# Sums of squares from GpSimd to VectorE, and half of the attention's probability scaling from VectorE to ScalarE

## The chip, the core and the metric

The kernel is one launch on one core of a Trainium2 chip. The metric is device microseconds of that launch, the median of several runs. A second source is one profiled execution, whose trace says when each instruction ran, what it waited for and which TensorE clock was granted. Engines are called as the profile calls them: PE is TensorE's matrix multiply and PEld its weight load, DVE is VectorE, ACT is ScalarE, POOL is GpSimd, SP is SyncE, which issues the DMAs. Columns of 128 partitions by W elements are written 128xW; everything here is float32.

## The reference, cut to what matters

A two-layer streaming encoder step on 1024 prompt frames and 32 sample frames (1056 columns), model width 1024. Layer 0 is a gated linear recurrence (HGRN2) and a SwiGLU feed-forward network; layer 1 is sliding-window attention with sinks and a second feed-forward network. Every sub-layer has a normalization before and after it. The change touches two computations:

```python
def rms_norm(x, w):
    xf = x.astype(F32)
    y = xf * lax.rsqrt(jnp.mean(xf * xf, axis=-1, keepdims=True) + NORM_EPS)
    return (y * w.astype(F32)).astype(x.dtype)
...
    p = jnp.exp(s - m)
    denom = jnp.sum(p, axis=-1, keepdims=True) + jnp.exp(sink - m)
    return jnp.einsum('bnkgqs,bnskd->bnqkgd', p / denom, v.astype(F32))
```

The first is a mean of squares over 1024 features, the second the division of the attention's exponentials by their sum.

## The kernel before, in words

Activations lie feature-major: eight tiles of 128 features, each with the columns of one of three blocks b of 384, 384 and 288 columns. Weights come by DMA as 128x1024 units; ACT rounds each to a high part `wh` (L102, or L98 with a scale per partition) and DVE takes the rest as a low part `wl` (L103, L99). Activations are split the same way into `xh` (ACT, L217 or L220) and `xl` (DVE, L218 or L221). A product then takes three passes on PE, high by high, high by low and low by high: L141 and L153 for projections, L416 and L141 in the first half of a feed-forward network, L507 in its second half. Products land in tiles tagged `mm`, of which there are four in PSUM.

**Sums of squares.** `sq_acc` (L176) is called once for each of the eight feature tiles of a block. The first call squares straight into an accumulator `acc` (ACT, L178). Each of the other seven squares into a scratch tile `q` (ACT, L181) and adds `q` to `acc` on POOL (L182). When all eight are in, `rnorm` (L184) sums over the 128 partitions with a matmul by ones (L188) and takes an inverse root with short ACT and DVE steps (L191, L192, L163 to L171). There are 24 such sums, so 168 adds: in `xload` (the input's pre-norm, three blocks), in `outproj` (six), in `postnorm` where a next norm follows (nine), and in the last loop of `ffn` (six, L593). In `postnorm`, each tile is scaled (L251), the residual is added (L252), the result split (L217, L218) and squared. In the last loop of `ffn`, a product tile is added into `mix` from PSUM (L592) and then squared.

**Attention.** `att_s` (L1249) handles one KV head g, its four query heads and one chunk of 128 (or 32) queries: 36 chunks. PE makes the scores (L1272, masks L1282), DVE takes row maxima (L1285, L1290, L1291), ACT exponentiates the four heads with row sums (L1294) and the sink (L1296), DVE adds the sink (L1297), takes the reciprocal (L1298) and multiplies all four heads at once by it, broadcast along the keys (L1299). `att_t` (L1303) then transposes the four heads on PE in the order 0 to 3 (L1312), ACT and DVE copy the transposes out (L1317, L1319), and `att_v` (L1322) multiplies by the values (L1330) and splits the result (L1332, L1333). The loop at L1392 calls `att_s` for chunk u, some projection work from the plan, and only then `att_t` and `att_v` for chunk u-1.

**Order.** The program writes tile operations; the order of each engine's queue is planned when it is built, from the dependencies, the order written and the builder's own estimates of durations, and then stays fixed. Each engine works through its queue in order. `rnorm`'s matmul is tied into PE's queue behind the last dense matmul written before it (`after_dense`, L156), so that PE waits there if the sum is not ready.

```python
        with after_dense():
            nc.tensor.matmul(ps[:, :W], ones, acc[:, :W], start=True, stop=True)
```

Of the kernel before, what the change touches and what calls it, by code (L numbers as in the profile page):

```python
# [13 lines left out]
AF = mybir.ActivationFunctionType  # L14
# [45 lines left out]
def build(nc, tc, I, O):  # L60
    ctx = ExitStack()
    mult, add, sub, mn = ALU.mult, ALU.add, ALU.subtract, ALU.min
# [20 lines left out]
    def tmp(bufs=4):  # L83
        return tp.tile([128, 384], F32, tag="tmp", name="tmp", bufs=bufs)
# [91 lines left out]
    def sq_acc(acc, W, src, first):  # L176
        if first:
            nc.scalar.activation(acc[:, :W], src, AF.Square)  # L178
        else:
            q = tmp()  # L180
            nc.scalar.activation(q[:, :W], src, AF.Square)  # L181
            nc.gpsimd.tensor_tensor(acc[:, :W], acc[:, :W], q[:, :W], add)  # L182

    def rnorm(acc, dst, W, ps=None):  # L184

# [37 lines left out]
    def postnorm(b, mix, acc, w2, xold, wnext, spill, yout, done, more=None, full=None):  # L223
# [25 lines left out]
        for k in range(KT):  # L249
            m = mix[:, k, :]  # L250
            nc.vector.scalar_tensor_tensor(m, m, pcol(w2, k), rb2[:, :W], mult, mult)  # L251
            nc.vector.tensor_tensor(m, m, xos[k][:, :W], add)  # L252
            load()
            if yout is None:
                if full is None:
                    put_x(b, k, m, xs, wnext)
                sq_acc(nacc, W, m, k == 0)
            if k % 2:
                nc.sync.dma_start(dst[:, k - 1:k + 1, :], mix[:, k - 1:k + 1, :])
                if k < KT - 1:  # L260
                    yield
# [962 lines left out]
    with tc.tile_pool(name="aps", bufs=1, space=PSUM, reuse_waits="tile") as aps:  # L1224
# [24 lines left out]
        def att_s(b, g, jl):  # L1249
            j = 3 * b + jl  # L1250
            samp = j == 8
            rows = 32 if samp else 128
            qs = slice(jl * 128, jl * 128 + rows)
            kb = kbs[b]
            if samp:
                keys = [(kc, 0, 128), (kb, 384, 32)]
                vals = [(vc, 128), (vts[8], 32)]
                lo, kend = 0, 160
            elif j == 0:
                keys, vals, lo, kend = [(kb, 128, 128)], [(vts[0], 128)], 128, 256  # L1260
            else:
                keys, vals, lo, kend = [(kb, jl * 128, 256)], [(vts[j - 1], 128), (vts[j], 128)], 0, 256
# [25 lines left out]
            rs = ap2.tile([128, 4], F32, tag="rs", name="rs", bufs=2)  # L1288
# [3 lines left out]
            P = ap2.tile([128, 4, 256], F32, tag="P", name="P", bufs=2)  # L1292
            for hh in (0, 2, 1, 3):
# [2 lines left out]
            nc.scalar.activation(es[:rows], es[:rows], AF.Exp)  # L1296
            nc.vector.tensor_tensor(rs[:rows], rs[:rows], es[:rows], add)  # L1297
            nc.vector.reciprocal(rs[:rows], rs[:rows])  # L1298
            nc.vector.tensor_tensor(P[:rows, :, lo:kend], P[:rows, :, lo:kend],  # L1299
                                    rs[:rows].unsqueeze(2).broadcast_to([rows, 4, kend - lo]), mult)  # L1300
            return dict(b=b, g=g, rows=rows, qs=qs, vals=vals, lo=lo, P=P)

        def att_t(c):  # L1303
# [76 lines left out]
        for b in range(NB):  # L1380
            if b == 1:
                kload(2)
                close(rpc)
                mbc, mb = pool("mb1", "right")

                def mtag(b):
                    return f"mixb{b}"

                mbs[:] = [mb, mb, None]
            os[b] = newx(b)  # L1390
            prev = None
            for u in range(13):  # L1392
                c = att_s(b, u // 3, u % 3) if u < 12 else None
                if u % 3 == 0 and u > 0 and order:
                    qload()
                for f, n in plan[b].get(u, ()):
                    go(f, n)
                if prev is not None:
                    att_t(prev)
                    att_v(prev)  # L1400
                prev = c
# [112 lines left out]
```

## Time and profile before

| | |
|---|---|
| median of 3 runs (lowest, highest) | 2544.05 us (2542.91, 2549.28) |
| the profiled execution's own time | 2548.6 us |
| its span, first to last instruction | 2546.8 us |
| PE busy | 2469.6 us (97%) |
| DVE busy | 1722.0 us (68%) |
| ACT busy | 1101.2 us (43%) |
| POOL busy | 457.5 us (18%) |
| mean granted TensorE clock | 0.988 |

The chain of waits follows the work that ended last back to its releasers; a group is all instructions of one line, engine and shape; "idle before" is an engine's idle time just ahead of an instruction, with what ended it. A window row gives, for one stretch: its length, then the busy time and count of PE, PEld, DVE, ACT and POOL, the granted clock (1.00 is full speed), the DMA share and GB/s. A timeline row gives start, duration, engine, line, operation, tiles, shapes, count and the idle time before it; consecutive instructions of one kind are merged into one row.

### The profile page before, as it was taken

The page shows a single profiled execution, that of the slowest core. Times are in us where ns is not written, and L with a number is a line of the kernel's source. Part 1 is how long each engine was busy: PE and PEld are TensorE (multiplying, and loading weights), DVE is VectorE, ACT ScalarE, POOL GpSimd, SP SyncE. Part 2 cuts the span into 40 slices and gives each one's busy share as a digit, 9 for nine tenths or more (in the row PEclk, how much of TensorE's full clock was granted, in tenths as well). Part 3 has the DMA queues.
Part 4 walks back from the last instruction along what each step waited for, and adds up shares of the span by engine and source line. Part 5 has one row for each costly group of instructions (what it writes and reads, how often), then busy time and mean ns, then how long its engine had stood idle before and what let it go on. Part 6 is the DMA issues. An engine that isn't in the chain of part 4 may idle for free.

```text
span 2546.8 us, 44040 instructions
## 1 busy us (share of the span) xinstructions
PE 2469.6 (97%) x17124; PEld 2373.7 (93%) x17124; DVE 1722.0 (68%) x3510; ACT 1101.2 (43%) x2395; POOL 457.5 (18%) x644
## 2 busy tenths in 40 slices
PE   7999998999999999999998999999999999999997
PEld 7999998998899999999998997777999999999997
DVE  8788789888776666643467747787776666652456
ACT  6555565666533333341344424565533333342333
POOL 4443444332300000000033321121300000000012
PEclk9999999999999999999999999998999999999998
DMA  5233334343422222242445542332422222252455
GB/s 171 91 101 99 115 110 138 124 135 107 156 72 82 80 77 76 78 166 77 150 158 165 181 128 63 86 120 70 162 80 76 76 76 77 77 177 76 147 168 156
DMA packets 124153, 287.98 MB, mean 113 GB/s; under 512 B 13432, under 2 KB 68632, under 8 KB 123944
## 3 DMA queue, kind: packets, MB, share of 16 engines
q1 hardware_dynamic: 123944, 285.17, 34.9%
q8 instruction: 134, 2.20, 0.3%
q14 instruction: 75, 0.61, 0.1%
HBM read 237.25 MB, written 48.07 MB: 112 GB/s over the span
## 4 chain that ended last, share of the span: by engine, by line
PE 74%; DVE 12%; DMA 5%; ACT 4%; issue 3%; POOL 1%; SPq 0%; POOLq 0%; DVEq 0%; ACTq 0%
PE mm L141 23%; PE mm L507 18%; PE mm L416 14%; PE c L416 6%; PE mm L153 5%; DVE wl L103 2%; PE sc L1272 2%; PE pav L1330 1%; ACT wh L102 1%; PE ptp L1312 1%; DVE wl L99 1%; DMA wst<-in_wfq 1%; DMA xl<-g 1%; DVE mixb L252 1%; DMA xo<-in_x 1%
## 5 line engine op out<-in xcount | busy, mean ns | idle before, releaser
L141 PE MATMUL mm<-xh,wh 128*128 128x384 f32 (+1 forms) x1968 | 632.9, 322 | 11.1 <-ACT xh L220 7.5
L141 PE MATMUL mm<-xh,wl 128*128 128x384 f32 (+1 forms) x1968 | 624.3, 317 | 5.5 <-DVE wl L99 3.0
L141 PE MATMUL mm<-xl,wh 128*128 128x384 f32 (+1 forms) x1968 | 627.1, 319 | 2.0 <-DVE xl L221 1.3
L182 POOL TENSOR_TENSOR acc<-acc,tmp 128x384 f32<-128x384 f32 (+1 forms) x168 | 211.3, 1262 | 1693.7 <-ACT tmp L181 1669.4
L103 DVE TENSOR_TENSOR wl<-wst,wh 128x1024 fp32r<-128x1024 f32 (+1 forms) x301 | 379.3, 1264 | 145.0 <-ACT wh L102 144.4
L102 ACT CAST wh<-wst 128x1024 fp32r<-128x1024 f32 (+1 forms) x301 | 313.6, 1046 | 343.5 <-PE mm L507 198.9
L141 PEld LDWEIGHTS mm<-xh,wh 128*128 128x128 f32 x1968 | 372.8, 190 | 20.9 <-ACT xh L220 7.5
L141 PEld LDWEIGHTS mm<-xh,wl 128*128 128x128 f32 x1968 | 373.0, 190 | 13.8 <-issue 5.6
L141 PEld LDWEIGHTS mm<-xl,wh 128*128 128x128 f32 x1968 | 372.6, 189 | 13.2 <-issue 4.7
L507 PE MATMUL mm<-xh,wl 128*128 128x384 f32 (+1 forms) x768 | 247.1, 322 | 4.7 <-DVE wl L103 4.7
L507 PE MATMUL mm<-xh,wh 128*128 128x384 f32 (+1 forms) x768 | 247.1, 322 | 0.0
L507 PE MATMUL mm<-xl,wh 128*128 128x384 f32 (+1 forms) x768 | 247.0, 322 | 0.0
L153 PE MATMUL mm<-wh,xh 128*128 128x256 f32 (+1 forms) x648 | 189.1, 292 | 3.2 <-DVE tmp L1130 2.2
L153 PE MATMUL mm<-wh,xl 128*128 128x256 f32 (+1 forms) x648 | 185.0, 285 | 0.0
L153 PE MATMUL mm<-wl,xh 128*128 128x256 f32 (+1 forms) x648 | 184.6, 285 | 0.0
L400 ACT CAST sh<-sr 128x512 fp32r<-128x512 f32 x144 | 89.5, 622 | 174.5 <-PE mm L416 146.5
L507 PEld LDWEIGHTS mm<-xh,wl 128*128 128x128 f32 x768 | 144.5, 188 | 5.2 <-DVE wl L103 5.2
L507 PEld LDWEIGHTS mm<-xl,wh 128*128 128x128 f32 x768 | 144.4, 188 | 0.0
L507 PEld LDWEIGHTS mm<-xh,wh 128*128 128x128 f32 x768 | 144.4, 188 | 0.0
L153 PEld LDWEIGHTS mm<-wh,xh 128*128 128x128 f32 (+1 forms) x648 | 119.9, 185 | 6.3 <-DVE tmp L1130 2.4
L153 PEld LDWEIGHTS mm<-wh,xl 128*128 128x128 f32 (+1 forms) x648 | 120.0, 185 | 0.7
L153 PEld LDWEIGHTS mm<-wl,xh 128*128 128x128 f32 (+1 forms) x648 | 119.9, 185 | 0.5
(283 smaller groups left out, 5144.4 us busy)
## 6 DMA issues: line engine op xcount, KB each, us to landing
wst<-in_wfo SPq DMA_DIRECT2D x92, 512.0 KB
wst<-in_wfi SPq DMA_DIRECT2D x88, 512.0 KB
wst<-in_wfq SPq DMA_DIRECT2D x47, 512.0 KB
g<-u SPq DMA_DIRECT2D x72, 192.0 KB
wst<-in_wi SPq DMA_DIRECT2D x24, 512.0 KB
wst<-in_wg SPq DMA_DIRECT2D x24, 512.0 KB
wst<-in_wao SPq DMA_DIRECT2D x24, 512.0 KB
xl<-g SPq DMA_DIRECT2D x32, 384.0 KB
```

The source lines that it names most:

```text
L99: nc.vector.scalar_tensor_tensor(wl[:, s], st[:, s], pcol(name, k0 + k), wh[:, s].bitcast(F32), mult, sub)
L102: nc.scalar.copy(wh[:, s], st[:, s])
L103: nc.vector.tensor_tensor(wl[:, s], st[:, s], wh[:, s].bitcast(F32), sub)
L141: last_mm[0] = nc.tensor.matmul(ps[:, :W], w, x, start=i == 0, stop=i == n - 1)
L153: last_mm[0] = nc.tensor.matmul(ps[:rows, :256], x, w, start=i == 0, stop=i == n - 1)
L182: nc.gpsimd.tensor_tensor(acc[:, :W], acc[:, :W], q[:, :W], add)
L252: nc.vector.tensor_tensor(m, m, xos[k][:, :W], add)
L400: nc.scalar.copy(h, r)
L416: last_mm[0] = nc.tensor.matmul(ps[:, :384], a, c, start=start and k == i == 0, stop=k == 3 and i == 2, skip_group_check=True)
L507: last_mm[0] = nc.tensor.matmul(ps[:, :W], a, c[:, q, :], start=start and q == i == 0, stop=stop and q == f - 1 and i == 2, skip_group_che ...
L1272: nc.tensor.matmul(pss[pr][:rows, pi, off:off + n], qts[b, g][rsl, pi, qs], kt_[rsl, g, k0:k0 + n], start=pi == 0 and off == lo, stop=samp ...
L1312: nc.tensor.transpose(ptp[:n, hh * rows:hh * rows + rows], P[:rows, hh, off:off + n], ident[:rows, :rows])
```

## The change

The add of a square to the accumulator is issued on DVE instead of POOL, at all 168 places. In the attention, DVE multiplies heads 0 and 1 by the reciprocal in one instruction of half the width, and ACT does heads 2 and 3, one instruction each, with the reciprocal as its scale per partition. Nothing else differs.

```diff
@@ -179,7 +179,7 @@
         else:
             q = tmp()
             nc.scalar.activation(q[:, :W], src, AF.Square)
-            nc.gpsimd.tensor_tensor(acc[:, :W], acc[:, :W], q[:, :W], add)
+            nc.vector.tensor_tensor(acc[:, :W], acc[:, :W], q[:, :W], add)
@@ -1296,8 +1296,10 @@
             nc.scalar.activation(es[:rows], es[:rows], AF.Exp)
             nc.vector.tensor_tensor(rs[:rows], rs[:rows], es[:rows], add)
             nc.vector.reciprocal(rs[:rows], rs[:rows])
-            nc.vector.tensor_tensor(P[:rows, :, lo:kend], P[:rows, :, lo:kend],
-                                    rs[:rows].unsqueeze(2).broadcast_to([rows, 4, kend - lo]), mult)
+            nc.vector.tensor_tensor(P[:rows, 0:2, lo:kend], P[:rows, 0:2, lo:kend],
+                                    rs[:rows, 0:2].unsqueeze(2).broadcast_to([rows, 2, kend - lo]), mult)
+            for hh in (2, 3):
+                nc.scalar.activation(P[:rows, hh, lo:kend], P[:rows, hh, lo:kend], AF.Copy, scale=rs[:rows, hh:hh + 1])
             return dict(b=b, g=g, rows=rows, qs=qs, vals=vals, lo=lo, P=P)
```

## The prediction

> **What bounds the kernel now.** I read the page first, then the waits of PE, the groups by shape, the chain around PE's longest wait, the timeline beside it, and the windows for the granted clock.
>
> ```profile
> span 2546.8 us, 44040 instructions
> PE 2469.6 (97%) x17124; PEld 2373.7 (93%) x17124; DVE 1722.0 (68%) x3510; ACT 1101.2 (43%) x2395; POOL 457.5 (18%) x644
> ```
>
> PE is the bound: 2546.8 - 2469.6 leaves 77 us in which it does nothing, and part of that is the start and the tail. No change on DVE, ACT or POOL can give more than PE's holes and the time that PE runs at a lower clock behind them. So the question is which holes this change fills or opens. PE's waits say which of them touch the two edits:
>
> ```profile
> PE mm L188 <- POOL acc L182: 10.1, 3, 7.1
> PE mm L507 <- DVE wl L103: 4.9, 3, 3.0
> PE ptp L1312 <- DVE P L1299: 3.0, 5, 1.2
> ```
>
> The columns are microseconds in total, times, and the longest. 10.1 us are waits for the sum of squares that POOL finishes, 3.0 us for the attention's product, and 4.9 us for a weight's low part on DVE, which any load on DVE's queue moves.
>
> **The change, part by part: the prices.** The groups give what is removed and what comes in its place:
>
> ```profile
> L182 POOL TENSOR_TENSOR acc<-acc,tmp 128x384 f32<-128x384 f32 x112 | 153.1, 1369 | 1554.6 <-ACT tmp L181 1531.8 <-ACT acc L178 21.2
> L182 POOL TENSOR_TENSOR acc<-acc,tmp 128x288 f32<-128x288 f32 x56 | 58.7, 1049 | 139.0 <-ACT tmp L181 137.6
> L465 DVE TENSOR_TENSOR u<-u,tmp 128x384 f32<-128x384 f32 x36 | 20.1, 558 | 3.5
> L1299 DVE TENSOR_TENSOR P<-P,rs 128x1024 f32<-128x1024 f32 x28 | 36.3, 1298 | 0.3
> L1299 DVE TENSOR_TENSOR P<-P,rs 128x512 f32<-128x512 f32 x4 | 2.8, 689 | 0.1
> L98 ACT ACTIVATE wh<-wst,pv 128x256 fp32r<-128x256 f32 x160 | 70.7, 499 | 57.9 <-PE mm L141 25.0 <-DMA wst<-in_wq 12.6 <-DMA wst<-in_wao 8.5
> L102 ACT CAST wh<-wst 128x1024 fp32r<-128x1024 f32 x299 | 312.4, 1049 | 341.9 <-PE mm L507 198.9 <-PE mm L141 56.8 <-PE mm L416 43.5
> ```
>
> Line 182 takes 212 us of POOL, 1.37 and 1.05 us apiece. The same add on DVE costs 0.56 us for 384 columns (L465, also two operands in SBUF) and, by width, about 0.46 for 288. That is 112 x 0.56 + 56 x 0.46 = 88 us of busy time added to DVE.
>
> DVE gets most of it back, because the two engines hold each other up:
>
> ```profile
> 1780.24 1.02 DVE L252 TENSOR_TENSOR mixb<-mixb,xo 128x384 f32<-128x384 f32 x2
> 1784.06 2.47 DVE L252 TENSOR_TENSOR mixb<-mixb,xo 128x384 f32<-128x384 f32 x2
> 1786.78 5.28 POOL L182 TENSOR_TENSOR acc<-acc,tmp 128x384 f32<-128x384 f32 x4 [0.67 <-ACT tmp L181]
> ```
>
> Two residual adds take 1.02 us where POOL is idle (0.51 each back to back) and 2.47 beside POOL's adds, 0.72 more each. POOL's adds beside DVE take 1.32 each. I went through the timeline for every DVE instruction that lies beside a line-182 add and took its excess over the median of the same shape where POOL is idle: 297 instructions, 67 us. The first and the last of them with an excess of half a microsecond or more are these:
>
> ```profile
> 9.85 1.89 DVE L221 SCALAR_TENSOR_TENSOR xl<-mixb,pv,xh 128x384 fp32r<-128x384 f32 x2
> 2517.55 1.63 DVE L252 TENSOR_TENSOR mix<-mix,xo 128x384 f32<-128x384 f32 x2
> ```
>
> So the adds cost DVE 88 and free 67 us: 21 us net in 2547. I take that as nothing on the path by itself; the PE work beside it, 97% busy, is the cover. Without cover the bounds are +21 and, if DVE's freed time falls where PE waits for it and the adds fall elsewhere, -4.9 (the whole row of PE's waits for L103).
>
> The Trainium skill has a rule for this pair: in "SBUF — State Buffer", section "Who interferes with whom", a DVE instruction with two SBUF inputs and a GpSimd instruction that reads SBUF exclude each other, and the later one is blocked for the whole of the other. By that rule the freed DVE time would be as much as line 182's whole 212 us. The rows show 0.72 us lost against an add of 1.32, so the sum stays with the counted 67.
>
> **What the removal does on the path.** PE's longest wait, 7.1 us, is a `rnorm` in the last loop of layer 0's feed-forward network. The chain of waits, in order of time (start, duration, what):
>
> ```profile
> 1331.63 2.03 DVE wl L103
> ...
> 1337.65 0.52 ACT tmp L181
> ...
> 1338.98 1.00 POOL acc L182
> 1339.99 0.07 issue
> 1340.06 1.86 POOL acc L182
> 1341.92 0.04 issue
> 1341.96 1.65 PE mm L188 x2
> ```
>
> PE stands from 1334.85 (1341.96 less 7.11). The square is done at 1338.17 and POOL's adds end at 1341.92. On DVE two adds are 1.0 us; a weight conversion that is put ahead of them adds 1.2 to 2.0. So the matmul starts between 1339.2 and 1341.2, that is 0.8 to 2.8 us earlier; I take 2.2, nearer the free end, because the conversion no longer meets POOL. The part of the wait ahead of 1338 stays: DVE's backlog there loses POOL's interference and gains the adds, which is even. The other two waits, and the tail:
>
> ```profile
> 652.48 3.50 POOL L182 TENSOR_TENSOR acc<-acc,tmp 128x384 f32<-128x384 f32 x3 [1.18 <-ACT tmp L181]
> 653.54 0.91 PE L188 MATMUL mm<-acc,ones 128*128 128x384 f32 x2 [1.01 <-POOL acc L182]
> 2530.68 0.79 POOL L182 TENSOR_TENSOR acc<-acc,tmp 128x288 f32<-128x288 f32 x1 [4.05 <-ACT tmp L181]
> ```
>
> At 653 PE waits 1.01 us for adds of 1.17; at 0.51 each nearly all of it goes, 0.9. In the tail nothing else runs, so 0.79 becomes 0.46: 0.3 us, the only certain gain. Together 3.4 us.
>
> **The attention.** The product over four heads takes 1.30 us, over half the width 0.69. ACT's two instructions, by the L98 row (same width, a scale per partition), are 0.50 each. Per chunk DVE loses 0.6 and ACT gains 1.0, some 20 and 35 us over 36 chunks. The new wait: ACT's queue stands until DVE's reciprocal is there, and behind it stand the next chunk's exponentials, the copies and the weight casts. The path from reciprocal to the finished product goes from 1.3 to 0.7 for the heads that PE transposes first and to about 1.0 plus a hop for the other two. PE starts transposing right behind the product:
>
> ```profile
> 1700.65 1.20 DVE L1299 TENSOR_TENSOR P<-P,rs 128x1024 f32<-128x1024 f32 x1
> 1702.00 1.07 PE L1312 MATMUL ptp<-ident,P 128*128 128x128 f32 x8 [0.68 <-DVE P L1299]
> ```
>
> So each of the five waits (3.0 us in all) can shrink by 0.4, which is 2.0 us. A short wait matters more through the clock:
>
> ```profile
> 1342.00:1348.00 6.00, 6.00 (x17) 5.39 (x18) 0.92 (x2) 1.85 (x3) 0.86 (x1) 0.51 0.27 89
> 1525.00:1775.00 250.00, 242.60 (x1577) 182.47 (x1575) 189.87 (x399) 141.66 (x466) 37.51 (x29) 0.99 0.28 86
> 1650.00:1675.00 25.00, 23.54 (x156) 17.07 (x154) 18.03 (x33) 14.60 (x44) 4.88 (x3) 1.00 0.30 91
> 1752.00:1762.00 10.00, 9.64 (x46) 6.97 (x47) 7.23 (x16) 5.23 (x16) 1.00 (x1) 0.66 0.36 114
> 1773.00:1783.00 10.00, 8.73 (x49) 7.77 (x50) 6.79 (x15) 2.78 (x7) 0.00 (x0) 0.66 0.09 26
> ```
>
> The clock is the third number from the end. Behind the 7.1 us hole PE runs at 0.51 for 6 us and loses 2.9; that hole stays longer than 4 us, so this loss stays. At the attention's end two stretches at 0.66 lose 3.4 us each; the second follows the longest of the five waits for the product (1.2 us). Holes of 1.5 us in sum at 1650 to 1675 left the clock at 1.00. With a little less wait at these two places each stretch has an even chance to go: 3.4 us taken, 0 and 6.8 as bounds. ACT stays far from full: 141.7 of 250 us, with 35 more 177.
>
> **Sum.** 3.4 (sums of squares) + 2.0 (product) + 3.4 (clock) = 8.8 us. The profiled execution would go from 2548.6 to 2539.8. It stood 4.55 above the median of 2544.05, and the same 8.8 us taken from the median give 2535.2. About 0.3% (7.6 us) is what a measurement of this kernel can tell from no change, so the forecast is barely a visible gain.
>
> **The rivals.**
> *No change.* The adds on DVE are queued behind weight conversions, which wait for ACT's casts, so the wait for L188 only changes its releaser. For it: POOL's row above idles 1532 us for the square, not for itself. Then only 0.9 + 0.3 remain: 2542.8. Chance 0.23.
> *More than I count.* Hold-ups between the two engines set PE's long waits; then all 10.1 us go, with the 2.9 of clock behind them, the 3.0 of the product and both stretches, 6.8: 22.8 us, 2521. Against it: the chain above starts in DVE's own queue. Chance 0.14.
> *Slower: DVE held by the square.* DVE works in order; an add that waits for ACT's square holds whatever is behind it, among that the emptying of PSUM (L592). ACT itself is held by casts that wait for PE:
>
> ```profile
> ACT wh L102 <- PE mm L507: 198.9, 53, 10.5
> 1303.65 24.96 PE mm L507 x144
> ```
>
> In the last loop a product tile takes 12 + 24 matmuls, at 24.96/144 each 6.2 us, and there are four tiles. POOL could wait as long as it liked. On DVE it decides from the point at which the hold passes 6.2 us: at the longest 10.5 that is a hole of 4.3 plus 2.9 of clock. Two of them, less the 1.2 of the sure gains, make +13.2: 2557. Chance 0.11.
> *Slower: ScalarE's heads come last.* The Trainium skill's "ScalarE: Activation LUTs", section "Rules for kernel authors", says to put multiplications on VectorE and not on ScalarE. Here two heads cost ACT 1.0 and DVE 0.69. Where a cast (1.05 us, the L102 row) stands ahead of them, the product is that much later, and PE has no slack. With a third of the chunks, 12 x 1.05 = 12.6, less the 3.4 of the sums: 2553. It decides where ACT's second head ends over 1.3 us behind the reciprocal. Chance 0.10.
>
> **How the numbers follow.** My forecast has 0.42. By the bounds of its terms it runs from 3.4 + 3.0 + 6.8 = 13.2 us (2531) down to 0.8 + 0.9 + 0.3 = 2.0 (2542); I put 0.34 of it below 2536.4, a visible gain, and 0.08 above. Faster is 0.34 + 0.14 = 0.48, within 0.3% 0.08 + 0.23 = 0.31, slower 0.11 + 0.10 = 0.21. What widens everything is the order: it is planned anew for all engines when durations move between them, and it is not the written one:
>
> ```profile
> 16.10 0.53 ACT L220 ACTIVATE xh<-xo,pv 128x288 fp32r<-128x288 f32 x1
> 22.20 0.62 ACT L220 ACTIVATE xh<-mixb,pv 128x384 fp32r<-128x384 f32 x1
> ```
>
> Block 2 (288 columns), written far later, is served ahead of block 1. A reshuffle may open or close holes of 2 us, each with up to 3.4 of clock, anywhere; three such either way are 16 us. The range runs from below the second rival, 2517, to between the two slower ones, 2556.
>
> **What would show it.** Right: line 182 on DVE at about 0.56 us, the residual adds beside it back near 0.51, DVE's busy total up by little (88 - 67 - 20), no wait of PE for POOL's sum, the wait near 1335 at about 5 us, the tail's add 0.3 us shorter, five or fewer short waits for the product. Wrong: new waits of L188 or L507 on DVE over 5 us with ACT's square as DVE's releaser, PE's transposes waiting for ACT's product, more stretches of low clock, or a gain far beyond 10 us in stages that hold neither edit.

## The result, and the profile after

The changed kernel takes 2512.36 us (median of 4 runs, 2509.75 to 2513.35), the kernel before 2545.43 us beside it (4 runs, 2542.91 to 2549.28). The ratio is 0.9867, 95% interval 0.985 to 0.9884: 33 us faster, where 8.8 were forecast, and 4.6 us below the forecast's range. Measured once more beside other runs, the changed kernel took 2514.54 us (2509.79 to 2522.84), ratio 0.9875 (0.9847 to 0.9903).

The profiled execution took 2509.75 us, the fastest of its four, where the profile of before came from an execution near the slow end of its runs; so the two traces differ by 38.8 us of span, about 6 more than the medians do. The page of after, its first lines:

```profile
span 2508.0 us, 43904 instructions
PE 2455.1 (98%) x17124; PEld 2367.2 (94%) x17124; DVE 1707.5 (68%) x3678; ACT 1130.2 (45%) x2467; POOL 243.3 (10%) x476
```

DVE does 168 instructions more than before and is busy for 14.5 us less. PE has the same 17124 matmuls and is busy for 14.5 us less: its mean granted clock was 0.993 in place of 0.988. PE's waits after (us in total, times, longest), the rows that answer to those of the prediction:

```profile
PE mm L188 <- DVE acc L182: 2.7, 2, 1.6
PE mm L507 <- DVE wl L103: 2.4, 2, 1.8
PE ptp L1314 <- ACT P L1302: 0.5, 1, 0.5
PE ptp L1314 <- DVE P L1299: 0.4, 2, 0.2
```

10.1 us of waits for the sums have become 2.7, of which 1.6 stand in the tail; 4.9 for a weight's low part have become 2.4; 3.0 for the attention's product have become 0.9. The moved line itself (duration in ns, least, median, most; and what ended DVE's idle time before it, us and times):

```profile
L182 DVE TENSOR_TENSOR acc<-acc,tmp x168: 442/549/756, 8.5 to 2492.3; 128x384 f32<-128x384 f32 x112, 128x288 f32<-128x288 f32 x56
...
  ACT tmp L181: 13.2, 19
```

The add costs 0.55 us, and DVE stood only 13.2 us for ACT's squares in the whole kernel.

Where the time went is seen by cutting both traces at the same instructions. Before, four of eight stages (first mixer with the start of the feed-forward network; second half of that network; attention; the stretch from attention's end into the next network). A row is from:to, length, then busy us and count of PE, PEld, DVE, ACT, POOL, then clock, DMA share, GB/s:

```profile
0.00:746.69 746.69, 714.32 (x6085) 688.80 (x6086) 616.37 (x1668) 427.95 (x1053) 278.11 (x499) 0.99 0.37 119
...
1123.75:1396.20 272.45, 259.31 (x1592) 256.92 (x1590) 144.88 (x185) 100.92 (x161) 47.16 (x33) 0.98 0.42 139
...
1519.03:1777.68 258.65, 251.25 (x1624) 189.67 (x1623) 193.73 (x407) 145.06 (x477) 39.51 (x31) 0.98 0.28 86
1777.68:1896.75 119.07, 115.91 (x718) 114.12 (x718) 93.65 (x155) 56.43 (x108) 23.83 (x21) 0.97 0.37 121
```

After, the same four, with the projections (the third row) for a later experiment:

```profile
0.00:733.63 733.63, 709.56 (x6085) 687.46 (x6086) 611.59 (x1731) 427.64 (x1053) 203.68 (x436) 0.99 0.38 121
...
1110.68:1373.41 262.73, 258.36 (x1591) 255.83 (x1590) 145.99 (x220) 102.39 (x162) 2.31 (x2) 0.99 0.45 146
1373.41:1494.95 121.54, 117.72 (x770) 115.92 (x769) 73.83 (x163) 40.06 (x98) 27.89 (x28) 0.99 0.51 160
1494.95:1741.66 246.71, 244.81 (x1625) 187.01 (x1624) 180.18 (x428) 172.62 (x549) 9.47 (x10) 1.00 0.29 90
1741.66:1858.72 117.06, 114.60 (x719) 112.52 (x718) 93.50 (x177) 57.00 (x108) 0.00 (x0) 0.99 0.38 123
```

The first stage is 13.1 us shorter, the second half of the feed-forward network 9.7, attention 11.9. The second half of the other network (2273.81 to the end before) holds 21 of the moved adds and does not gain: 273.0 us before, 272.2 after, 274.2 in the second profile of the changed kernel. The two stages of 377 us that lie between are the same to 0.01 us: PE has no hole there. In the second half of the feed-forward network DVE is busy for the same time before (144.9) and after (146.0), and yet the stage is shorter. That is the riddle of this case.

The place of the longest wait, before (timeline: start, duration, what; rows of DVE and of POOL):

```profile
1330.33 1.37 DVE L251 SCALAR_TENSOR_TENSOR mix<-mix,pv,rb 128x384 f32<-128x384 f32 x1
1331.63 2.03 DVE L103 TENSOR_TENSOR wl<-wst,wh 128x1024 fp32r<-128x1024 f32 x1
1333.58 1.36 DVE L218 TENSOR_TENSOR xl<-mix,xh 128x384 fp32r<-128x384 f32 x1
...
1328.87 5.66 POOL L182 TENSOR_TENSOR acc<-acc,tmp 128x384 f32<-128x384 f32 x3 [3.88 <-ACT tmp L181]
1337.41 5.45 POOL L182 TENSOR_TENSOR acc<-acc,tmp 128x384 f32<-128x384 f32 x4 [2.88 <-ACT tmp L181]
```

And after, the same operations:

```profile
1317.56 1.14 DVE L251 SCALAR_TENSOR_TENSOR mix<-mix,pv,rb 128x384 f32<-128x384 f32 x2
...
1320.02 1.21 DVE L103 TENSOR_TENSOR wl<-wst,wh 128x1024 fp32r<-128x1024 f32 x1
1321.16 0.55 DVE L218 TENSOR_TENSOR xl<-mix,xh 128x384 fp32r<-128x384 f32 x1
1321.62 0.55 DVE L182 TENSOR_TENSOR acc<-acc,tmp 128x384 f32<-128x384 f32 x1
```

Beside POOL's three adds of 5.66 us, DVE's scaling took 1.37 (two take 1.14 after), the weight's low part 2.03 (1.21), the split 1.36 (0.55). The 7.1-us hole of PE behind this is now 1.08 us, and the clock no longer falls:

```profile
1322.00:1334.00 12.00, 10.92 (x68) 10.57 (x68) 9.18 (x15) 5.71 (x9) 0.00 (x0) 1.00 0.67 210
```

### The profile page after: what moved, and what is told of

It is laid out like the page before. It is cut to its first block, busy times and chain, and to the rows that moved or that the text cites. A ratio compares the mean times of both kernels' runs of the same rounds, so it can differ in the third digit from the quotient of the medians.

```text
span 2508.0 us, 43904 instructions
## 1 busy us (share of the span) xinstructions
PE 2455.1 (98%) x17124; PEld 2367.2 (94%) x17124; DVE 1707.5 (68%) x3678; ACT 1130.2 (45%) x2467; POOL 243.3 (10%) x476
## 4 chain that ended last, share of the span: by engine, by line
PE 79%; DVE 10%; DMA 5%; ACT 4%; issue 2%; POOL 1%; SPq 0%; DVEq 0%; ACTq 0%; POOLq 0%
PE mm L141 27%; PE mm L507 17%; PE mm L416 15%; PE mm L153 6%; PE c L416 6%; PE sc L1272 2%; DVE wl L103 2%; PE pav L1332 1%; PE ptp L1314 1%; DMA wst<-in_wfo 1%; ACT wh L102 1%; DVE acc L182 1%; DVE wl L99 1%; DMA xl<-g 1%; DMA wst<-in_wk 1%
## 5 line engine op out<-in xcount | busy, mean ns | idle before, releaser
L141 PE MATMUL mm<-xh,wh 128*128 128x384 f32 (+1 forms) x1968 | 630.4, 321 | 10.4 <-ACT xh L220 7.0
L103 DVE TENSOR_TENSOR wl<-wst,wh 128x1024 fp32r<-128x1024 f32 (+1 forms) x301 | 368.1, 1226 | 137.7 <-ACT wh L102 137.3
L507 PE MATMUL mm<-xh,wl 128*128 128x384 f32 (+1 forms) x768 | 247.3, 322 | 2.4 <-DVE wl L103 2.4
L507 PE MATMUL mm<-xh,wh 128*128 128x384 f32 (+1 forms) x768 | 247.3, 322 | 0.0
L507 PEld LDWEIGHTS mm<-xh,wl 128*128 128x128 f32 x768 | 144.9, 189 | 2.8 <-DVE wl L103 2.8
L399 DVE TENSOR_TENSOR sr<-wst 128x512 f32<-128x512 f32 x72 | 49.5, 688 | 74.9 <-DMA wst<-in_wfi 74.9
```

The source lines that it names most:

```text
L103: nc.vector.tensor_tensor(wl[:, s], st[:, s], wh[:, s].bitcast(F32), sub)
L141: last_mm[0] = nc.tensor.matmul(ps[:, :W], w, x, start=i == 0, stop=i == n - 1)
L399: nc.vector.tensor_tensor(r, x, y, op)
L507: last_mm[0] = nc.tensor.matmul(ps[:, :W], a, c[:, q, :], start=start and q == i == 0, stop=stop and q == f - 1 and i == 2, skip_group_che ...
```

## The experiments

Theory H: GpSimd's adds hold VectorE up, and these hold-ups, more than VectorE's load, make PE's holes. The rivals: only the column sum's wait for the last GpSimd add counts (L), the gain is mostly attention's (A), the buffer of the square is held too long (B), any GpSimd instruction beside VectorE slows it (C), GpSimd's slow adds at the end of each sum count (E), the planner's new order makes the time (R). P and S are two prices for VectorE's load, T and V two outcomes of carrying the trade on. Idle adds and fills write a tile whose values are used nowhere; on GpSimd it is a bfloat16 tile. Times are medians in us; stages are from the profiled execution.

| run | time (lowest, highest) | ratio to before (95%) | first stage | network's 2nd half | attention | DVE busy |
|---|---|---|---|---|---|---|
| before, first measurement | 2545.43 (2542.91, 2549.28) | | 746.7 | 272.5 | 258.7 | 1722.0 |
| after | 2512.36 (2509.75, 2513.35) | 0.9867 (0.985, 0.9884) | 733.6 | 262.7 | 246.7 | 1707.5 |
| after, again | 2514.54 (2509.79, 2522.84) | 0.9875 (0.9847, 0.9903) | 736.3 | 262.7 | 247.0 | 1709.3 |
| squares only | 2528.61 (2528.19, 2530.68) | 0.9924 (0.9909, 0.9938) | 739.6 | 260.3 | 260.0 | 1723.8 |
| attention only | 2534.44 (2531.52, 2540.33) | 0.9948 (0.993, 0.9965) | 747.4 | 273.1 | 247.9 | 1699.0 |
| idle GpSimd add on the square | 2548.05 (2542.68, 2551.83) | 0.9997 (0.9987, 1.0007) | 752.8 | 270.5 | 247.3 | 1768.7 |
| both halves on VectorE | 2523.11 (2520.33, 2526.26) | 0.9901 (0.9886, 0.9916) | 741.4 | 259.3 | 254.7 | 1726.3 |
| short read, then idle GpSimd add | 2549.14 (2547.41, 2557.45) | 1.0008 (0.9995, 1.0021) | 754.7 | 271.1 | 248.9 | 1755.1 |
| short read alone | 2520.02 (2514.6, 2521.73) | 0.9884 (0.9869, 0.99) | 741.4 | 262.0 | 247.1 | 1709.2 |
| short read, then fill | 2518.34 (2516.55, 2520.86) | 0.9882 (0.9867, 0.9897) | 740.2 | 263.9 | 246.7 | 1710.0 |
| rotation on VectorE too | 2509.94 (2505.88, 2511.1) | 0.9846 (0.9831, 0.986) | 740.2 | 261.4 | 247.5 | 1713.6 |
| nothing but fills on GpSimd | 2518.5 (2513.71, 2518.52) | 0.9881 (0.9859, 0.9902) | 748.6 | 259.9 | 246.9 | 1753.9 |
| idle VectorE adds, early | 2533.98 (2531.69, 2535.29) | 0.9945 (0.9925, 0.9965) | 754.7 | 262.5 | 247.4 | 1754.4 |
| idle VectorE adds, in place | 2525.61 (2523.71, 2533.51) | 0.9929 (0.9907, 0.9951) | 736.4 | 267.1 | 253.7 | 1741.7 |
| one network's sums only | 2536.67 (2530.19, 2543.56) | 0.9958 (0.9944, 0.9973) | 743.4 | 260.5 | 255.4 | 1719.2 |
| last two adds only | 2542.0 (2539.53, 2545.21) | 0.9981 (0.9968, 0.9995) | 746.7 | 269.7 | 254.7 | 1727.7 |
| sums on GpSimd, new order | 2548.41 (2543.3, 2553.47) | 1.0001 (0.9989, 1.0013) | 742.1 | 267.3 | 261.3 | 1722.8 |
| sums on VectorE, old order | 2528.81 (2524.11, 2534.86) | 0.9915 (0.9893, 0.9937) | 744.2 | 263.4 | 254.7 | 1726.1 |

Two stages vary between executions, and smaller differences there say nothing. The first took 733.6 to 741.4 us where its instructions and their order are the changed kernel's, 743.4 to 747.4 where they are those of before. Attention took 254.7 to 261.3 us in the six kernels that have it as before, 246.7 to 248.9 in ten executions that have the change's (253.7 with VectorE's load added in place).

Part of attention's spread is the clock. The run with one network's sums only has attention's instructions in the order of before and PE stands idle there for about the same time (7.6 us against 7.4), with the same two holes of 1.0 and 1.2 us near the end. Yet the clock fell once less, and the stage is 3.2 us shorter:

```profile
1504.73:1760.14 255.41, 247.81 (x1624) 187.23 (x1623) 193.53 (x407) 145.20 (x477) 39.52 (x31) 1.00 0.29 87
```

### Each edit alone

**Squares only.** The kernel before with this alone:

```diff
-            nc.gpsimd.tensor_tensor(acc[:, :W], acc[:, :W], q[:, :W], add)
+            nc.vector.tensor_tensor(acc[:, :W], acc[:, :W], q[:, :W], add)
```

> Only the adds of the squares go to DVE; the attention's product is as before. Theory H (hold-ups: POOL's adds and DVE's two-operand instructions stop each other, and the holes of PE and the low clock behind them come from that): the stages outside the attention come out as in the changed kernel (about 27 us of span less than before), the attention somewhat shorter too, because POOL's adds leave it: total 2516 to 2524 us. Theory L (only the wait of rnorm's matmul for the last POOL add counts): 3 to 6 us less than before, about 2540. Theory A (the gain is mostly the attention's product): within 8 us of before.

It gave 2528.61, 19.4 us less than the 2548.04 of before in the same measurement: toward H, though 4.6 us above its band. Its rows for the second half of the network and for attention:

```profile
1116.67:1376.99 260.32, 256.53 (x1592) 254.45 (x1590) 143.77 (x217) 102.22 (x162) 1.98 (x2) 1.00 0.46 145
...
1499.66:1759.64 259.98, 254.95 (x1632) 191.81 (x1631) 195.81 (x430) 146.16 (x478) 9.98 (x10) 0.97 0.28 85
```

12 us go in the one, nothing in the other, where DVE's load stays at 196 us and the clock is as low as before: H's second forecast, a shorter attention too, did not come true.

**Attention only.** The changed kernel with the add back on `nc.gpsimd`.

> Only the attention's product is split between DVE and ACT; the squares are added on POOL as before. Theory H: the attention's stage loses 4 to 9 us (waits for the product and at least one of its two stretches of low clock), nothing moves outside it: 2535 to 2541 us. Theory A: 20 us or more less than before, about 2522. If ScalarE's heads come last: 2546 or more.

2534.44, 13.6 us less than before, just below H's band. The same two stages:

```profile
1124.45:1397.52 273.07, 260.34 (x1591) 257.62 (x1590) 144.84 (x186) 101.47 (x161) 47.10 (x33) 0.98 0.43 139
...
1520.20:1768.06 247.86, 244.81 (x1632) 188.27 (x1631) 175.91 (x411) 173.02 (x550) 31.59 (x31) 1.00 0.29 89
```

Now attention is 10.8 us shorter and the network is not. 19.4 + 13.6 = 33.0 us is the whole (33.1): the edits add up, and nothing shows that they help each other.

**Both halves on VectorE.** The changed kernel, heads 2 and 3 as a second half-width instruction of DVE:

```diff
-            for hh in (2, 3):
-                nc.scalar.activation(P[:rows, hh, lo:kend], P[:rows, hh, lo:kend], AF.Copy, scale=rs[:rows, hh:hh + 1])
+            nc.vector.tensor_tensor(P[:rows, 2:4, lo:kend], P[:rows, 2:4, lo:kend],
+                                    rs[:rows, 2:4].unsqueeze(2).broadcast_to([rows, 2, kend - lo]), mult)
```

> The changed kernel, but heads 2 and 3 are multiplied on DVE as a second instruction of half the width instead of on ACT. If the attention gains because DVE is relieved by ACT: its stage goes from 247 back to about 252 us and the total to about 2518. If it gains only because the first two heads are ready earlier: no change, 2511 to 2514.

2523.11, 10.8 us more than the changed kernel (8.6 more than its second measurement) and 5.5 less than with the squares only. So more than half of what the attention's edit brings goes with the relief of DVE. The stage, and PE's waits for the product:

```profile
1501.70:1756.41 254.71, 250.17 (x1636) 189.31 (x1635) 198.44 (x466) 146.60 (x478) 9.02 (x10) 1.00 0.29 87
```

```profile
PE ptp L1314 <- DVE P L1299: 2.0, 5, 0.9
```

Attention is 8.0 us longer than after, with DVE at 198 instead of 180 us. But its window holds 11 more matmuls (1636 against 1625), which the new plan puts there; attention and the stretch behind it together are 5.8 us longer (369.6 against 363.8). So ACT's taking the load is worth 6 to 8 us in this stage. What is left, 4 to 8 us, falls to the first two heads' being ready earlier, to the new order of the queues in this stage, and to its spread; no run parts these. The five waits for the product (3.0 us before) are still 2.0 here.

The Trainium skill's rule to use VectorE and not ScalarE for multiplications ("ScalarE: Activation LUTs", "Rules for kernel authors") is given there per element. Per element this trace agrees: two heads take 0.73 us on VectorE and 2 x 0.52 on ScalarE after the change. For this kernel's time the other choice is better, for ACT is busy for 173 of 247 us in this stage, and PE waits for its two instructions only once, 0.5 us.

### Hold-up, buffer or load

**Idle GpSimd add on the square.** The changed kernel, and behind each of the 168 adds:

```diff
+            nc.gpsimd.tensor_tensor(idle, q[:, :288], q[:, :288], add)
```

> The changed kernel with one more instruction at each of the 168 places: POOL adds 288 columns of the square to themselves and writes them to a tile that nobody reads, so the output is unchanged and no sum waits for POOL; the order of PE, ACT and DVE is the same as in the changed kernel, instruction for instruction. Theory H: DVE's busy time grows by 40 us or more and most of the gain outside the attention is lost again, 2527 to 2536 us. Theory L: within 4 us of the changed kernel, 2512 to 2516, since rnorm's matmul never waits for POOL. A theory that the new order of the queues made the gain: also no change, 2512.

2548.05: the whole gain is lost to instructions that compute nothing, with DVE held for 61 us more. But the trace of this run shows a second cost, ACT's next square waiting for POOL to give its buffer back:

```profile
1331.38 0.53 ACT L183 ACTIVATE tmp<-mix 128x384 f32<-128x384 f32 x1 [2.51 <-POOL idle L185]
```

**Short read, then an idle add; its control; and a fill.** Three kernels part the two costs. The first line alone is the control, which gives the buffer back early; the second is the idle add on a tile that no other engine uses; the third writes and does not read:

```diff
+            nc.gpsimd.tensor_tensor(idle[:, :8], q[:, :8], q[:, :8], add)     # all three
+            nc.gpsimd.tensor_tensor(idle, idle, idle, add)                    # the first run
+            nc.gpsimd.memset(idle, 0.0)                                       # the third run
```

> The changed kernel with two idle GpSimd instructions behind each of the 168 squares: an add of 8 columns that reads the square (and so gives its buffer back early), and then an add of 288 columns that reads and writes only a tile that nothing else uses. In the run with one idle add of 288 columns on the square itself (2548.05 us) ScalarE's next square was seen to wait for GpSimd to give the buffer back, so that run mixed two costs. Theory H (GpSimd's adds hold VectorE up, and that alone costs PE): 2535 to 2550 us, VectorE's total near 1765 us against 1707.5. Rival B (the square's buffer was held too long, GpSimd being the slow reader): 2510 to 2520 us, even if VectorE's total rises. Between 2522 and 2533: both have a share.

> The control of the run above: the changed kernel with only the add of 8 columns on GpSimd behind each square, no add of 288 columns. Theory H: 2510 to 2517 us, VectorE's total within 12 us of 1707.5, since GpSimd is busy for some 0.2 us at each place. Rival B: also near 2512, since the buffer comes back soon. If it lands at 2520 or above, the mere hand-over (one more engine that a buffer waits for) costs, and neither theory in this form holds.

> As the run with the short add and the 288-column add, but the second GpSimd instruction fills the idle tile with zeros: it writes SBUF and reads nothing. Theory H in the form that the Trainium skill's page "SBUF - State Buffer", section "Who interferes with whom", gives (only GpSimd instructions that read SBUF exclude VectorE's two-input instructions): 2510 to 2517 us, VectorE's total within 12 us of the run with the short add alone. Rival C (any GpSimd instruction beside VectorE slows it): 2518 us or more, in proportion to the fill's duration.

2549.14, 2520.02 and 2518.34. The control lies above H's band and 5.5 to 7.7 us above the two medians of the changed kernel, but only 2 to 4 us by the ratios to the kernel before, whose intervals overlap: whether the hand-over to a third engine costs time is not shown. Beyond that, H holds and B falls: the idle add costs 29 us with no buffer to wait for, and the fill costs nothing. A new plan is not the reason: the traces show DVE's and ACT's instructions in one and the same order in the changed kernel and in all four runs with idle GpSimd instructions. The engines' totals, first with the idle add, then the control, then the fill:

```profile
PE 2470.3 (97%) x17124; PEld 2376.9 (93%) x17124; DVE 1755.1 (69%) x3678; ACT 1129.8 (44%) x2467; POOL 475.2 (19%) x813
```

```profile
PE 2457.5 (98%) x17124; PEld 2367.8 (94%) x17124; DVE 1709.2 (68%) x3678; ACT 1130.8 (45%) x2467; POOL 343.8 (14%) x645
```

```profile
PE 2458.5 (98%) x17124; PEld 2370.4 (94%) x17124; DVE 1710.0 (68%) x3678; ACT 1128.5 (45%) x2467; POOL 398.4 (16%) x813
```

DVE issues the same 3678 instructions in all three. They take 45.9 us longer beside adds that read, and 0.8 us longer beside fills. By the Trainium skill ("SBUF — State Buffer", "Who interferes with whom") a VectorE instruction with two SBUF inputs contends with a GpSimd instruction that reads SBUF, and not with one that only writes it. The fill bears that out.

How the 46 us of DVE reach PE is seen in PE's waits, with the idle adds and in the control:

```profile
PE mm L141 <- DVE wl L103: 12.1, 8, 3.4
PE mm L193 <- DVE acc L185: 10.7, 4, 5.9
PE pt L963 <- POOL K L946: 5.4, 2, 2.9
```

```profile
PE mm L141 <- DVE wl L103: 4.2, 5, 1.6
PE mm L192 <- DVE acc L185: 4.7, 3, 1.9
PE pt L962 <- POOL K L945: 4.9, 2, 3.4
```

PE waits 7.9 us longer for weights' low parts and 6.0 longer for sums, both from DVE, and only 0.5 longer for POOL. So delays of POOL's own small instructions behind the idle adds are not what PE waits for directly; that they act through other engines in the first stage is not ruled out. In all, PE stands for 17.4 us more and is busy for 12.8 us more with the same matmuls.

**Idle VectorE adds.** As much of DVE's time, but as load in its own queue. The first form used `idle` alone, the second reads the square:

```diff
+            nc.vector.tensor_tensor(idle, idle, idle, add)                    # early
+            nc.vector.tensor_tensor(idle, q[:, :144], q[:, :144], add)        # in place
```

> The changed kernel with an idle add of 144 columns on VectorE itself behind each of the 168 sums (some 0.28 us each by 442 ns for 288 columns and 549 ns for 384, 47 us in all): as much of VectorE's time as GpSimd's idle adds took from it by holding it up (1755.1 less 1709.2 = 46 us), but as load in its own queue and with no GpSimd beside it. The hold-ups cost 29 us of span (2548.05 to 2549.14 against 2520.02). Theory P (a microsecond of VectorE is worth the same, however it is lost): 2512.4 + 29 = 2541, between 2533 and 2548. Rival S (only hold-ups cost so much, load in the queue is absorbed): 2512 to 2522, which is what the prediction took for load. Between them: 2523 to 2532, load costs about half of what a hold-up does.

2533.98, but the run does not answer its question: the adds depended on nothing, and the planner put all 168 into the first 245 us, as their row shows (duration, then first and last start):

```profile
L186 DVE TENSOR_TENSOR idle<-idle x168: 256/307/645, 1.2 to 244.3; 128x144 f32<-128x144 f32 x168
```

> The idle add of 144 columns on VectorE once more (0.31 us each in the run before, 52 us in all), now reading the square, so that it stays behind each of the 168 sums; in the run before, all 168 stood within the first 245 us, because they depended on nothing, and so loaded the first stage alone. Theory P (a lost microsecond of VectorE costs the same, as load or as a hold-up): as with GpSimd's idle adds against their control, 9 us more in the second half of the first feed-forward network, 6 in the stretch behind attention, 5 to 13 in the first stage: 2533 to 2548 in all. Rival S (load in the queue is absorbed outside the first stage, hold-ups are not): 63 of the 168 stand in the first stage, 20 us of load at the 15 to 21 us for 47 that the run before paid, so 6 to 9 us, and the other stages within 3 us of the changed kernel's: 2515 to 2524.

2525.61, 13.3 us more than the changed kernel (11.1 more than its second measurement, 14 to 16 by the ratios) for 34.2 us more of DVE: between P and S, and neither. A microsecond more of DVE's busy total costs 0.39 as load (0.32 to 0.46 by the other readings), and 29.1/45.9 = 0.63 as a hold-up. The load's own row (busy, mean ns, idle before) shows that its 50.4 us, which overlap with their neighbours, cost 0.26 for each:

```profile
L185 DVE TENSOR_TENSOR idle<-tmp 128x144 f32<-128x144 f32 x168 | 50.4, 300 | 0.1
```

But this run has a new plan: some 230 of DVE's 3510 other instructions stand elsewhere in its queue, 56 of them in attention, and attention alone is 7.0 us longer. So that load is cheaper than a hold-up is not shown cleanly. In the second half of the network, where 15 stand elsewhere, the two prices are alike. With the idle GpSimd adds, their control, and load in place:

```profile
1131.73:1402.87 271.14, 259.58 (x1591) 256.99 (x1590) 155.22 (x216) 101.76 (x160) 46.39 (x66) 0.98 0.44 140
```

```profile
1118.41:1380.40 261.99, 256.36 (x1592) 254.45 (x1590) 143.95 (x217) 102.40 (x162) 24.23 (x34) 1.00 0.46 144
```

```profile
1113.42:1380.51 267.09, 259.18 (x1592) 256.92 (x1590) 151.94 (x252) 102.13 (x162) 5.71 (x2) 0.99 0.45 145
```

9.2 us of the stage for 11.3 of DVE, and 4.4 (against the changed kernel's 262.73) for 6.0. So this stage, with DVE busy little over half of the time, hides only a fifth to a quarter of what DVE loses.

### Where, and by which cause

**One network's sums only.** The kernel before, with DVE for the adds of the first feed-forward network and of the norm behind it (L593 with `L == 0`, and L257 when called from `ffn`).

> The kernel before with only the sums of the first feed-forward network on VectorE (42 of 168: those of its output blocks and of the norm behind them); the others stay on GpSimd and attention is as before. If the gain of moving the sums is local, the second half of that network falls from 272.5 us to 260 to 264 with the 7.1-us wait ahead of its last column sum gone, the other stages stay within 3 us, and the whole is at 2532 to 2538. If the gain comes from elsewhere (one stage's delay given on to the next), that half stays above 267 and the whole above 2540.

2536.67, with the 12 us where they were expected (the profile is from one of its fastest executions):

```profile
1120.46:1380.92 260.46, 256.81 (x1591) 254.35 (x1590) 143.98 (x217) 102.31 (x162) 2.12 (x2) 1.00 0.46 146
```

Outside this network's second half and the projections behind it, DVE's queue keeps the order of before. The gain is local.

**Last two adds only.** Is it the slow end of POOL's chain of seven adds?

```diff
-            nc.gpsimd.tensor_tensor(acc[:, :W], acc[:, :W], q[:, :W], add)
+            (nc.vector if k > 5 else nc.gpsimd).tensor_tensor(acc[:, :W], acc[:, :W], q[:, :W], add)
```

> The kernel before, with only the last two of the seven adds of each sum of squares on VectorE (48 of 168); the first five stay on GpSimd, attention is as before. Moving all the sums left VectorE's load in the second half of the first feed-forward network unchanged (144.9 and 143.8 us) and yet shortened it by 12 us. Theory E (GpSimd's slow adds at the end of the chain of a sum, ahead of the column sum that PE waits for): nearly the whole gain is had with 48 adds, that half at 260 to 264 us, the whole at 2528 to 2535. Theory H (hold-ups all along): two sevenths of the gain and no more, that half at 267 to 272, the whole at 2540 to 2546.

2542.0: 3.9 us less than before, no more than H's share (two sevenths of 19.4 are 5.5), and the wait for the last column sum is still there, now on DVE's adds behind POOL's first five: 5.3 us in this network.

```profile
1123.76:1393.44 269.68, 258.82 (x1591) 256.16 (x1590) 148.37 (x195) 101.79 (x162) 36.41 (x25) 0.99 0.44 141
```

```profile
PE mm L189 <- DVE acc L183: 6.9, 2, 5.3
```

**The changed kernel again**, the control for the first stage.

> The changed kernel once more, as a control for the first stage: it took 733.6 us in the profile of the changed kernel and 739.6 to 741.4 in four experiments whose first stage has the same instructions. If that is spread between executions, the first stage comes out anywhere from 733 to 742 and the whole at 2509 to 2516; if the others differ in their order there, it stays at 733 to 735.

The first stage came out at 736.3: spread between executions, as the first reading had it.

**Engine or order.** Comparing the queues stage by stage shows that the plan is a new one in the stages that gain, and in attention, which does not; in the two stages of 377 us DVE's order is the old one. So each engine's adds were run with the other's order, the queues of all five engines pinned by edges that set order and wait for nothing:

```diff
+        for a, b in zip(seq, seq[1:]):
+            tc.add_manual_dep(b, a.name, mybir.DependencyInfo(mybir.DependencyClass.NoSync, mybir.DependencyReason.DATA),
+                              reason="order")
```

> The kernel before, sums on GpSimd, but every engine's queue pinned to the order that the planner gave to the kernel with the sums on VectorE (2528.61 us); only the adds themselves stand on GpSimd. Between the two plans 37 of some 187 VectorE instructions of the second half of the first feed-forward network stand elsewhere in the queue, and 144 of 1680 in the first stage. Theory H (the engine that adds makes the time): 2540 to 2550, that half at 267 to 273 us. Rival R (the new order makes the time, VectorE's load being the same): 2526 to 2534, that half at 259 to 264. In between: both have a share.

> The other corner: sums on VectorE, attention as before, and all other instructions of every engine pinned to the order of the kernel before (the adds stand where the planner puts them between these). Theory H: 2525 to 2533, as with the sums on VectorE and the new order (2528.61). Rival R: 2540 to 2555, the 3 to 7-us wait ahead of the last column sum of the first feed-forward network back.

2548.41 and 2528.81. With GpSimd 2547.33 (old order, measured beside them) and 2548.41 (new), with VectorE 2528.81 (old) and 2528.61 (new): the engine makes 19 us, the order nothing that shows. R falls for the whole. The network's second half, first with GpSimd and the new order, then with VectorE and the old one:

```profile
1119.12:1386.46 267.34, 257.79 (x1591) 255.54 (x1590) 148.28 (x186) 102.34 (x162) 43.52 (x33) 0.99 0.44 142
```

```profile
1121.21:1384.60 263.39, 257.94 (x1592) 255.88 (x1590) 144.69 (x220) 101.53 (x162) 0.00 (x0) 0.99 0.45 143
```

Here the new order is worth 3 to 5 us and the engine 7 to 9 (272.5, 267.3, 263.4, 260.3). PE's wait for the column sum falls from 7.1 us to 4.5 by the order alone, to 2.9 by the engine alone, and to 1.5 by both. Attention goes the other way: 260.0 and 261.3 us with the new order, 258.7 and 254.7 with the old one, so that nothing of the order's share is left in the whole. Each of these is one execution, and the first stage (746.7, 742.1, 744.2, 739.6 in the same sequence) varies too much to part the two.

### Can the trade be carried on?

**Rotation on VectorE too.** The changed kernel with L1125, L1133 and L1134 on `nc.vector`.

> The changed kernel with GpSimd's 40 remaining instructions of the rotation (41 us of GpSimd) on VectorE as well: some 40 x 0.55 = 22 us more for VectorE's queue, less the hold-ups beside them. Theory H: the same trade as the squares, whose move alone gained 19 us for 211 us of GpSimd, so 41/211 x 19 = 4 us: 2506 to 2510. Rival (VectorE's load is what counts, and the squares gained by their own chain of sums, which GpSimd worked through at 1.26 us each): 2512 to 2520, with no gain in the stage of the projections (121.5 us).

2509.94, the fastest of all, but its ratio's interval overlaps the changed kernel's: as a whole not shown to be faster. Its stage is, by 4.5 us, with PE's holes there down from 3.8 to 0.5 us:

```profile
1378.67:1495.70 117.03, 116.48 (x771) 114.47 (x769) 79.01 (x194) 39.90 (x98) 0.00 (x0) 1.00 0.55 169
```

**Nothing but fills on GpSimd.** That kernel, and in the first mixer:

```diff
-    V, KE = nc.vector, nc.gpsimd
+    V, KE = nc.vector, nc.vector
```

> The run with the rotation on VectorE (2509.94 us), and in addition the sixteen-odd kinds of small GpSimd instructions of the first mixer on VectorE, so that GpSimd keeps only fills: 200 us of GpSimd and its hold-ups leave, an estimated 100 us and more of own work come to VectorE, all in a stage of 734 to 740 us where VectorE was busy for 612. Theory T (the trade of the squares carries over: less hold-up is worth more than the added load): 2490 to 2505. Rival V (VectorE becomes the bound there): 2525 to 2560, with PE's waits of the first stage rising from 26 us to 40 and more.

2518.5, between the two theories, and 8.6 us slower than the run before:

```profile
0.00:748.58 748.58, 717.29 (x6084) 690.97 (x6085) 653.27 (x2139) 427.28 (x1053) 3.56 (x28) 0.98 0.38 119
```

DVE is at 653 us (612 in the run before) in the stage, which is 8.4 us longer. Here 200 us of GpSimd cost DVE less as hold-ups than as its own work, 41 us net: the trade stops.

## Why the prediction was wrong, point by point

**The step that failed** is "21 us net ... I take that as nothing on the path by itself", with its companion "The part of the wait ahead of 1338 stays: DVE's backlog there loses POOL's interference and gains the adds, which is even." The load was even, and better than even: 144.9 to 146.0 us in that half, 1722.0 to 1723.8 in the run with the squares alone. But even load did not mean even time: with DVE's instructions the same, 46 us of hold-ups cost 29 us. The squares were priced at 3.4 us and brought 19.4. The bounds for this term, +21 and -4.9, did not hold it either: the far bound was PE's row of waits for L103 alone, while a held-up DVE also delays residuals, splits and squares, and with them other waits of PE.

**The wait near 1335** was to be about 5 us; it is 1.08, and 2.9 where the order of before is kept, so the engine took 4.2 us off and the new order the rest. The reading of the chain ("the square is done at 1338.17") began too late. DVE's instructions ahead of that square were themselves held up, by the three adds from 1328.87 to 1334.53: scaling, low part and split took 4.76 us there, and some 2.3 after. These rows also bear on what the prediction made of 0.72 us lost against an add of 1.32, less than a full block. The split began at 1333.58 and ended at 1334.94, 0.41 us behind the end of the adds, and it takes 0.55 alone: here DVE was held until close to the add's end, and lost less than the add's length because it had begun later. The count of 67 stands all the same.

**The argument against the rival that came nearest.** "More than I count" had the right mechanism, at 2521 us and with a chance of 0.14. Against it stood "the chain above starts in DVE's own queue". It did; that queue was late because GpSimd held it. The rival's own sum, 22.8 us, counted only PE's waits that named the two edits and no others, and so left out nearly all of the first stage, where 63 of the adds stand.

**"A gain far beyond 10 us in stages that hold neither edit"** was to prove me wrong, and is not what happened: the stages that gained hold edits. The first stage lost 13.1 us between the profiles, 10.4 with the second execution of the changed kernel, and 7.6 between the means of three and five executions. It does hold adds, but I had given it 0.9 us.

**The attention** was 5.4 us and brought 13.6 in all, 11.9 in its stage. The waits were 2.0, from the five that name the product and its shorter path. That path alone, in the run with both halves on VectorE, took 1.0 off these waits. The larger part is DVE's relief, 0.6 us a chunk, which the prediction counted as load and did not price: PE's time without work fell from 7.4 to 1.9 us. The clock term was 3.4 with 6.8 as bound; PE's busy time fell by 6.4 with the same work. That both stretches of low clock went is in part luck: one of them is missing also in an execution with the attention of before.

**What held.** The add at 0.55 us (0.56 forecast). No wait of PE for POOL's sum. The tail's wait fell from 2.02 to 1.58, 0.44 us (0.3). The products on ACT took 23 us from DVE's total (20 forecast); but the sums were to add 21 to it and added 1.8, so hold-ups freed more than the 67 counted, or the adds overlapped with their neighbours. Two mishaps, DVE held by the square and ScalarE's heads last, did not happen: 13.2 us of idle before L182 in all, and 0.5 us for PE before ACT's heads. The third, a reshuffle of the order, did happen and cost or brought the whole nothing.

**What stays open.** By the measured prices 67 us of hold-ups at 0.63 are 42 us; 88 us of adds are 23 at 0.26 (by the row of the load in place) and up to 40 at 0.46 (by busy totals). That is 2 to 19 us of the 19.4. So the two prices carry the gain in part or in whole. That a microsecond of hold-up costs more than one of load is suggested by these totals and not shown, since the run with the load has another order; at one and the same order no run here has it. Nor is it parted how much of the gain is the hand-over through a third engine, or why the 21 adds in the second network's second half brought nothing.

## What to carry to other kernels

Where two engines hold each other up, do not set the freed time off against the added time, as if both were load: put an idle instruction on the suspected engine and read what the whole costs. Look for DVE instructions whose duration doubles beside another engine's, ahead of the longest wait and not only at its end. And try the trade piece by piece, reading the receiving engine's busy total. Moving the squares left DVE's total where it was (1722.0 and 1723.8 us) and paid; moving the first mixer's small instructions raised it by 41 us and did not. How busy DVE is did not decide by itself: in the first stage, at 83% (616 of 747 us), moving the squares made the stage shorter and moving the small instructions made it longer.

## What the runs showed of the hardware

A GpSimd add that reads 288 bfloat16 columns held VectorE for 45.9/168 = 0.27 us on the mean, though it lasts 0.86 us itself (median). 168 fills of 0.34 us cost VectorE 0.8 us in all, and 168 adds of 8 columns, 0.42 us each (median), 1.7 us. At the adds' price for each microsecond of GpSimd (45.9 for 147) the fills' 57 us would have cost 18 and the short adds' 102 us would have cost 32. So what holds VectorE up here is how much GpSimd reads, not how long it is busy.

A hole of PE can cost twice, and need not. In attention PE's time without work fell from 7.4 to 1.9 us, and with the clock at 1.00 in place of 0.98 its busy time, for the same work, fell by 6.4. But with the same holes in another execution the mean clock was 1.00 as well, and PE's busy time 3.4 us shorter.
